# Merge gates as Strassen's seven products over pairs of feature tiles, kept in DRAM, and the branch products in a stage of their own

## The chip, the core and the metric

One core of a Trainium2 chip runs the program once. TensorE (PE) multiplies a loaded 128x128 weight tile (LDWEIGHTS, the PEld rows) with up to 512 columns into a bank of PSUM; VectorE (DVE), ScalarE (ACT) and GpSimd (POOL) do the elementwise work; SyncE (SP) issues most DMAs. The metric is the device time of one execution in microseconds (us): the median of 3 runs of the kernel before is 1403.04, and the runs lie between 1402.95 and 1403.12.

## What is computed

The reference is one layer of a network with three branches over 1024 tokens of 1024 features. Everything is float32.

```python
y = x @ w_in                  # 1024 x 1024 x N_IN, cut into the inputs of the branches
ya = attention(...)           # branch A: 512 features
yb = spatial_gating(...)      # branch B: 512 features
yc = mlstm(...)               # branch C: 512 features
merged = sum(sigmoid(gate_b) * (y_b @ w_br_b) for b in (a, b, c))   # gate_b: the last 3 x 1024 columns of y
r = ALPHA * x + merged @ w_out
r = r + sigmoid(r @ ple_gate) * (p @ ple_w)
out = layernorm(r)
```

The change concerns the merge: the gates, 3072 features of `x @ w_in` for 1024 tokens, and the three products `y_b @ w_br_b`, 512 features to 1024 each.

## The kernel before

All activations lie with features on the partitions and tokens along the free axis. A product in float32 is made of pairs: every operand is split into a rounded part (`hi`, an ACT cast to float32r) and the rest (`lo`, a DVE subtraction), and three matmuls hi*hi, lo*hi and hi*lo add up in one PSUM bank. `load_w` (L84) loads a 512 KB weight tile into `wraw`, casts it (L92) and subtracts (L93); `split` (L97) does the same to an activation tile (L102, L103); `proj_half` (L109, its matmul is L116) then makes a 128x512 result with 3 x K matmuls, K the number of 128-row feature tiles: 24 for the 8 tiles of x, 12 for the 4 tiles of a branch. x is held as 8 hi and 8 lo tiles (`xh`, `xl`, the 16 buffers of tag `x`) from the start to the end of the merge.

The program runs through these parts in this order: loading x and the compressed keys (to about 55 us of the span), attention (branch A, with projections of A and B between its steps), the gating branch B and the mLSTM branch C (their working tiles lie in the pool `pq`, L603, opened when the pool of A is closed and closed at L824), the merge (L831 to L872), the output projection (L874), and the last gate with the layer norm (L899 to L979).

The merge has a loop over the 3 branches `b`. It splits the four tiles of the branch (L837, into the pool `pf`, which is opened at L832 where `pq` was), and for each of the 8 feature tiles `n` of the output makes two gate halves (`ps_g`, L850, 24 matmuls each, with a tanh on ACT, L852) and two branch halves (`ps_b`, L858, 12 matmuls each). DVE multiplies the two (L860, L862) and for the second and third branch POOL adds the result to `M[n]` (L863). At the end `M` is split into `mh`, `ml` (L869, L870), which the output projection reads. ya, yb and yc stay in SBUF until they are split: ya and yb are the 8 buffers of tag `y`, yc the 4 of the pool `ycp`.

The order in which an engine gets its instructions is set by a scheduler at build time: it takes the program in the order written as the priority, plays it through, and gives each engine the first instruction in that order whose inputs and buffers are there. Each engine then runs its list in order and waits on semaphores. A tile waits until a buffer of its tag is free; the tiles of a pool wait for all that was done with the pools that lay at its place before.

Of the kernel before, what the change touches and what calls it, by code (L numbers as in the profile page):

```python
# [45 lines left out]
def hybrid_kernel(ctx, tc, xT, pT, wfm, wvg, wtm, cmpw1, cmpw2, cpos, vecs, sgwT, sgb,  # L46
# [32 lines left out]
    # ---------------------------------------------------------------- constants  # L79
# [3 lines left out]
    # ---------------------------------------------------------------- weights  # L83
# [22 lines left out]
    # ---------------------------------------------------------------- x  # L106
    xh, xl = [], []

    def proj_half(po, w, half, hs, ls, K=KT, M=P):  # L109
        wh, wl = w  # L110
        s = slice(half * 512, half * 512 + 512)
        n = 3 * K
        i = 0
        for k in range(K):
            for a, b in ((wh, hs), (wl, hs), (wh, ls)):
                mm(po[:M, :], lhsT=a[:, k, :], rhs=b[k][:, s], start=(i == 0), stop=(i == n - 1))  # L116
                i += 1

    def proj_tok(po, ws, tt, n, hs, ls):
        s = slice(tt * P, tt * P + P)  # L120
        i = 0
        tot = 3 * KT
        for k in range(KT):
            wh, wl = ws[k // 4]
            for a, b in ((hs, wh), (hs, wl), (ls, wh)):
                mm(po[:, :n], lhsT=a[k][:, s], rhs=b[:, k % 4, :], start=(i == 0), stop=(i == tot - 1))
                i += 1

    def proj_tok256(src, hs, ls):
        """[tokens, 256] for all token tiles, two to a bank; yields the banks in order."""  # L130
        bank = [pj(), pj(), pst("st", 2), pst("st", 2)]
        for i in range(2):
            wh, wl = load_w(src[:, 4 * i:4 * i + 4, :], 4, 256)
            for tt in range(NT):
                s = slice(tt * P, tt * P + P)
                po = bank[tt // 2][:, tt % 2 * 256:tt % 2 * 256 + 256]
                for k in range(4):
                    for j, (a, b) in enumerate(((hs, wh), (hs, wl), (ls, wh))):
                        mm(po, lhsT=a[4 * i + k][:, s], rhs=b[:, k, :],  # L139
# [16 lines left out]
    def gelu2(dst, src, n):  # L156
        """dst = 2*gelu(src) with src in PSUM or SBUF."""
# [8 lines left out]
    def silu2(dst, src, n):  # L166
        """dst = 2*silu(src)."""
# [9 lines left out]
    # ================================================================ branch A  # L177
# [21 lines left out]
    def load_x(k, parts):  # L199
        raw = yp.tile([P, T], F32, tag="y", bufs=YB, name="xraw")  # L200
        xh.append(xp.tile([P, T], F32R, tag="x", bufs=16, name="xh"))
        xl.append(xp.tile([P, T], F32R, tag="x", bufs=16, name="xl"))
        for i in range(parts):
            load_cols(raw, xT[k], (xh[k], xl[k]), slice(i * T // parts, (i + 1) * T // parts))
            if k == 0 and i == 0:
                load_kv(1, 0, 2)
# [3 lines left out]
    load_x(1, 2)  # L210
    for kv in range(2):
        load_kv(kv, 2, 8)
    for k in range(2, KT):
        load_x(k, 1)
# [19 lines left out]
    # ---- key/value streams of the compressed branch, x consumed as it arrives  # L234
# [8 lines left out]
    for k in range(KT):  # L243
        for half in range(2):
            for kv, w in enumerate((wk, wv)):
                s = slice(half * 512, half * 512 + 512)
                for i, (a, b) in enumerate(((w[0], xh), (w[1], xh), (w[0], xl))):
                    mm(pkv[kv][half], lhsT=a[:, k, :], rhs=b[k][:, s], start=(k == 0 and i == 0),
# [36 lines left out]
    # ---- values (with a column of ones) and gate logits, token-major  # L285
# [11 lines left out]
    # ---- compression  # L297
# [48 lines left out]
    def prep_group(g):  # L346
# [5 lines left out]
        for n in "sw":  # L352
            vv.tensor_scalar_mul(d["KB" + n][64:128, 0:1], xl[-1][64:128, 0:1].bitcast(F32), 0.0)
# [45 lines left out]
    def attn_front(g, qb, d):  # L399
# [3 lines left out]
        # compressed branch  # L403
# [57 lines left out]
        # row maxima of the window and of the selection  # L461
# [137 lines left out]
    # ================================================================ branch B  # L599
    pa_ctx.close()  # L600
    ycp = pool("ycp")
# [10 lines left out]
    vb = [ycp.tile([P, 2, 512], F32, tag="yc", bufs=4, name="vb") for _ in range(4)]  # L612
# [3 lines left out]
    # ================================================================ branch C  # L616
    yc = []
    # gate rows, one (head, chunk) per partition
# [29 lines left out]
    vv.tensor_scalar(out=cm, in0=cm, scalar1=mp, scalar2=None, op0=OP.max)      # u  # L648
# [15 lines left out]
    # values with ones  # L664
# [8 lines left out]
    # gating branch: normalize, mix over the chunk, gate  # L673
# [33 lines left out]

    def conv_proj(i, nm):
# [20 lines left out]
    for h in range(NH_C):  # L729
        yc.append(ycp.tile([P, T], F32, tag="yc", bufs=4, name="yc"))  # L730
# [65 lines left out]
        # gates o and z  # L796
# [18 lines left out]
        for hf in range(2):  # L815
# [7 lines left out]
            vv.tensor_mul(yc[h][:, s], pt, oz[:, s])  # L823
    pq_ctx.close()  # L824
    if "yc" in dbg:
        for i in range(4):
            nc.sync.dma_start(dbg["yc"][i], yc[i])
# [3 lines left out]
    # ================================================================ merge  # L831
    pf = pool("pf")  # L832
    M = [pf.tile([P, T], F32, tag="M", bufs=8, name="M") for _ in range(8)]
    for b, ys in enumerate((ya, yb, yc)):
        yh, yl = [], []
        for i in range(4):
            h, l = split(ys[i], pf, "s", 8)  # L837
            yh.append(h)
            yl.append(l)
        for n in range(8):  # L840
            wg = wf(FM["mg"] + 8 * b + n)
            if n % 2 == 0:
                raw = wp.tile([P, 1024], F32, tag="wraw", bufs=2, name="wraw")
                nc.sync.dma_start(raw, wbr[b, n // 2])
                wb = [t.rearrange("p (k n) -> p k n", k=8) for t in split(raw, yp, "y", YB)]
            w = (wb[0][:, 4 * (n % 2):4 * (n % 2) + 4, :], wb[1][:, 4 * (n % 2):4 * (n % 2) + 4, :])
            ts = []
            for half in range(2):
# [244 lines left out]
```

## Time and profile before

| | us |
|---|---|
| median of 3 runs | 1403.04 |
| span of the profiled execution, from its first to its last instruction (the only time of its own on the page) | 1401.3 |
| PE busy | 1383.6 (99%) |
| DVE busy | 695.8 (50%) |
| ACT busy | 430.9 (31%) |
| POOL busy | 154.7 (11%) |
| HBM read and written | 80.1 MB, 57 GB/s over the span |

The rows below give times from the start of the span. Busy time of PE counts each matmul from its issue to its modelled end, so that the times of neighbours overlap; the distance between their starts is what a matmul takes of the engine.

### The profile page before, as it was taken

What the parts mean: (1) busy time and instruction counts of PE and PEld (TensorE: products, weight loads), DVE (VectorE), ACT (ScalarE), POOL (GpSimd) and SP (SyncE); (2) the same over time, 40 slices, a digit from 0 to 9 for tenths busy, and PEclk for the clock granted to TensorE, in tenths of its full rate; (3) what the DMA queues carried; (4) which work ended last, traced back from release to release, by engine and by line L of the source; (5) the groups of instructions that cost most, each with busy time, mean ns of one, the idle gap of its engine ahead of it and who ended that gap; (6) DMA issues with size and microseconds to landing.
All of it is one profiled execution on the core that took longest, in us unless ns stands there. A gap on an engine that the chain in (4) does not pass through costs nothing. (4 is left out here: it accounts for less than half of the span.)

```text
span 1401.3 us, 18726 instructions
## 1 busy us (share of the span) xinstructions
PE 1383.6 (99%) x7375; PEld 1174.8 (84%) x7375; DVE 695.8 (50%) x1719; ACT 430.9 (31%) x875; POOL 154.7 (11%) x177
## 2 busy tenths in 40 slices
PE   9999999999999999999999999999999999999997
PEld 7978888887888999988888888888888888888886
DVE  6247677436678544575575721131123232334755
ACT  6353434243332332132332311121112122224211
POOL 0011221101211000010110000001111111000312
PEclk9999999999999999999999999999999999999999
DMA  9031111111010021021121121111111112223211
GB/s 309 31 84 31 31 35 31 39 45 42 24 34 6 16 93 46 31 76 46 61 76 46 46 62 59 45 46 45 46 46 49 57 45 89 80 83 121 87 38 46
DMA packets 26872, 81.31 MB, mean 58 GB/s; under 512 B 3480, under 2 KB 6424, under 8 KB 26784
## 3 DMA queue, kind: packets, MB, share of 16 engines
q1 hardware_dynamic: 25824, 76.96, 16.8%
q0 software_dynamic: 960, 3.15, 1.0%
q8 instruction: 58, 0.95, 0.3%
q14 instruction: 30, 0.25, 0.1%
HBM read 75.84 MB, written 4.26 MB: 57 GB/s over the span
## 5 line engine op out<-in xcount | busy, mean ns | idle before, releaser
L116 PE MATMUL ps_pj<-xh,whi 128*128 128x512 f32 x544 | 217.5, 400 | 2.3 <-DVE QA L386 2.3
L93 DVE TENSOR_TENSOR wlo<-wraw,whi 128x1024 fp32r<-128x1024 f32 x74 | 91.1, 1230 | 253.6 <-ACT whi L92 253.4
L116 PE MATMUL ps_pj<-xh,wlo 128*128 128x512 f32 x544 | 216.7, 398 | 0.0
L116 PE MATMUL ps_pj<-xl,whi 128*128 128x512 f32 x544 | 214.9, 395 | 0.0
L116 PE MATMUL ps_g<-xh,whi 128*128 128x512 f32 x384 | 149.5, 389 | 0.0
L116 PE MATMUL ps_g<-xh,wlo 128*128 128x512 f32 x384 | 149.4, 389 | 0.0
L116 PE MATMUL ps_g<-xl,whi 128*128 128x512 f32 x384 | 149.4, 389 | 0.0
L520 PEld LDWEIGHTS ps_o<-V,pt 128*128 128x128 f32 x912 | 117.1, 191 | 11.9 <-ACT pt L500 3.5
L116 PEld LDWEIGHTS ps_pj<-xh,whi 128*128 128x128 f32 x544 | 102.3, 188 | 22.7 <-PE ps_pj L116 3.9
L116 PEld LDWEIGHTS ps_pj<-xl,whi 128*128 128x128 f32 x544 | 102.4, 188 | 18.7
L116 PEld LDWEIGHTS ps_pj<-xh,wlo 128*128 128x128 f32 x544 | 102.7, 189 | 17.5
L520 PE MATMUL ps_o<-V,pt 128*128 128x65 f32 x912 | 116.2, 270 | 0.4 <-POOL pt L502 0.3
L852 ACT ACTIVATE mth<-ps_g 128x512 f32<-128x512 f32 x48 | 28.7, 597 | 253.1 <-PE ps_g L116 250.4
L500 ACT ACTIVATE pt<-ps_st 128x512 f32<-128x512 f32 x114 | 65.7, 594 | 102.0 <-PE ps_st L498 98.4
L92 ACT CAST whi<-wraw 128x1024 fp32r<-128x1024 f32 x74 | 77.3, 1045 | 49.8 <-PE ps_st L139 25.0
L116 PEld LDWEIGHTS ps_g<-xh,whi 128*128 128x128 f32 x384 | 72.1, 188 | 15.0
L116 PEld LDWEIGHTS ps_g<-xh,wlo 128*128 128x128 f32 x384 | 72.1, 188 | 14.9
L116 PEld LDWEIGHTS ps_g<-xl,whi 128*128 128x128 f32 x384 | 72.1, 188 | 14.9
L863 POOL TENSOR_TENSOR M<-M,mth 128x512 f32<-128x512 f32 x32 | 43.0, 1343 | 370.9 <-DVE mth L862 207.0
L116 PE MATMUL ps_b<-sp_hi 128*128 128x512 f32 x192 | 74.7, 389 | 0.0
L116 PE MATMUL ps_b<-sp_hi,sp_lo 128*128 128x512 f32 x192 | 74.7, 389 | 0.0
L116 PE MATMUL ps_b<-sp_lo,sp_hi 128*128 128x512 f32 x192 | 74.7, 389 | 0.0
(323 smaller groups left out, 2665.7 us busy)
## 6 DMA issues: line engine op xcount, KB each, us to landing
wraw<-in_wfm_dram SPq DMA_DIRECT2D x58, 512.0 KB, 3.5
wraw<-in_wbr_dram SPq DMA_DIRECT2D x12, 512.0 KB, 3.2
wraw<-in_wtm_dram SPq DMA_DIRECT2D x8, 512.0 KB, 3.7
wraw<-in_wout_dram SPq DMA_DIRECT2D x8, 512.0 KB, 3.3
xr<-in_xT_dram SPq DMA_DIRECT2D x8, 512.0 KB, 5.0
graw<-in_pleg_dram SPq DMA_DIRECT2D x8, 512.0 KB, 3.3
out_dram<-rtok SPq DMA_DIRECT2D x14, 256.0 KB, 2.0
xraw<-in_xT_dram SPq DMA_DIRECT2D x6, 512.0 KB, 9.3
```

The costliest lines, as they stand in the source:

```text
L92: nc.scalar.copy(hi[:, c], raw[:, c])
L93: vv.tensor_sub(lo[:, c], raw[:, c], hi[:, c])
L116: mm(po[:M, :], lhsT=a[:, k, :], rhs=b[k][:, s], start=(i == 0), stop=(i == n - 1))
L500: act(pt.rearrange("p h q -> p (h q)"), sp, AF.Exp)
L520: mm(po[:, h * 65:h * 65 + 65], lhsT=pt[:, h, :], rhs=V[:, j, vi, :], start=(first and h == 0), stop=last, skip_group_check=True)
L852: act(t, pg, AF.Tanh, scale=0.5)
L863: nc.gpsimd.tensor_add(M[n][:, s], M[n][:, s], t)
```

## The change

x comes from the host in another layout (`xm`): each of its 8 tiles holds two neighbouring feature tiles for one half of the tokens, loaded in the same order and sizes as before. The tiles of ya, yb and yc are stored to DRAM (`ysc`, 12 stores of 512 KB) when their branch is done; yc now lies in `pq`, and the pool `ycp` is gone. After `pq` is closed come two stages in place of the merge loop.

The first stage makes all gates, two output tiles at a time (12 pairs, `q`), by Strassen's scheme in Winograd's form: the weights of a pair are a 2x2 matrix of blocks (output tile by half of the features), x a 2x2 matrix (half of the features by half of the tokens), and seven products of 4 feature tiles each (12 matmuls) take the place of eight. The sums of x blocks (`T1` to `T4`) are made and split once, before the first pair; the sums of weight blocks are made and split for every product (`total`, `left`). Three of the seven results are copied out of PSUM (`kept`) because later ones go on adding into the same bank. The tanh of each gate tile is stored to DRAM (`gsc`, 24 stores of 512 KB). The second stage loads the branch tiles and the gate tiles back and makes the branch products.

```diff
+    for i in range(4):
+        nc.sync.dma_start(ysc[0][i], ya[i])
...
-            vv.tensor_mul(yc[h][:, s], pt, oz[:, s])
+            vv.tensor_mul(yc[:, s], pt, oz[:, s])
+        nc.sync.dma_start(ysc[2][h], yc)
     pq_ctx.close()
...
+    pg_ = pg_ctx.enter_context(tc.tile_pool(name="pg", bufs=1))
+    def split_op(src, pl_, tg, bf):
+        hi = pl_.tile([P, T], F32R, tag=tg, bufs=bf, name="op_hi")
+        lo = pl_.tile([P, T], F32R, tag=tg, bufs=bf, name="op_lo")
+        nc.scalar.copy(hi, src)
+        vv.tensor_sub(lo, src, hi)
+        return hi, lo
...
+    for m in range(2):
+        raws.append([yp.tile([P, T], F32, tag="y", bufs=YB, name="xraw") for _ in range(4)])
+        for t, (mm_, j) in zip(raws[m], ((m, 0), (m, 1), (m + 2, 0), (m + 2, 1))):
+            nc.sync.dma_start(t, xm[mm_, j])
+    for m in range(2):
+        b11, b12, b21, b22 = raws[m]
+        vv.tensor_sub(b11, b12, b11)
+        right["T1"][m] = split_op(b11, pg_, "t", 12)
+    for m in range(2):
+        b11, b12, b21, b22 = raws[m]
+        nc.gpsimd.tensor_sub(b12, b22, b12)
+        vv.tensor_sub(b22, b22, b11)
+        right["T2"][m] = split_op(b22, pg_, "t", 12)
+    for m in range(2):
+        b11, b12, b21, b22 = raws[m]
+        right["T3"][m] = split_op(b12, pg_, "t", 12)
+    for m in range(2):
+        b11, b12, b21, b22 = raws[m]
+        vv.tensor_sub(b21, b21, b22)
+        right["T4"][m] = split_op(b21, xp, "x", 16)
...
+        def left(src):
+            hi = pg_.tile([P, 512], F32R, tag="sh", bufs=4, name="sh")[:, 0:w]
+            lo = pg_.tile([P, 512], F32R, tag="sl", bufs=4, name="sl")[:, 0:w]
+            nc.scalar.copy(hi, src)
+            vv.tensor_sub(lo, src, hi)
...
+        def product(bank, src, name, first):
+            l = left(src)
+            for k in range(K):
+                r = [t[:, k % 2 * 512:k % 2 * 512 + 512] for t in right[name][k // 2]]
+                for i, (a, b) in enumerate(((0, 0), (1, 0), (0, 1))):
+                    mm(bank, lhsT=l[a][:, k, :], rhs=r[b], start=first and k == 0 and i == 0,
+                       stop=k == K - 1 and i == 2, skip_group_check=True)
...
+        a = pst("pj", 2, "ps_a")
+        product(a, a11, "B11", True)
+        c1 = kept(a)
+        b = pst("st", 2, "ps_b")
+        s1 = total(a21, a22, OP.add)
+        product(b, s1, "T1", True)
+        c5 = kept(b)
+        s2 = total(s1, a11, OP.subtract)
+        product(a, s2, "T2", False)
+        c2 = kept(a)
+        product(b, total(a12, s2, OP.subtract), "B22", False)
+        done(0, 1, b, c2)
+        product(a, total(a11, a21, OP.subtract), "T3", False)
+        done(1, 1, a, c5)
+        c = pst("o", 2, "ps_c")
+        product(c, a12, "B21", True)
+        done(0, 0, c, c1)
+        product(a, a22, "T4", False)
+        done(1, 0, a, None)
+    for q in range(12):
+        raw = [wp.tile([P, 1024], F32, tag=tg, bufs=bf, name="mraw") for _ in range(2)]
...
+        def done(i, j, bank, kept):
+            if kept is not None:
+                vv.tensor_add(kept, bank, kept)
+                bank = kept
+            act(gt[i][:, j * 512:j * 512 + 512], bank, AF.Tanh, scale=0.5)
+        strassen(raw[0], raw[1], 4, right, done)
+        for i in range(2):
+            nc.sync.dma_start(gsc[2 * q + i], gt[i])
+    pg_ctx.close()
     pf = pool("pf")
-    for b, ys in enumerate((ya, yb, yc)):
+    for b in range(3):
         for i in range(4):
-            h, l = split(ys[i], pf, "s", 8)
+            raw = yp.tile([P, T], F32, tag="y", bufs=YB, name="yraw")
+            nc.sync.dma_start(raw, ysc[b][i])
+            h, l = split(raw, xp, "x", 16)
         for n in range(8):
-            wg = wf(FM["mg"] + 8 * b + n)
...
-                proj_half(pg, wg, half, xh, xl)
-                t = tp.tile([P, 512], F32, tag="ge_a", bufs=2, name="mth")
-                act(t, pg, AF.Tanh, scale=0.5)
+            t = yp.tile([P, T], F32, tag="y", bufs=YB, name="gt")
+            nc.sync.dma_start(t, gsc[8 * b + n])
...
-                pb2 = pst("o", 2, "ps_b")
+                pb2 = pst(("o", "pj", "st")[(2 * n + half) % 3], 2, "ps_b")
```

The raw weight tiles of a pair use the tags `wraw`, `whi` and `wlo` in turn. `mh` and `ml` and the later gate weights move to the buffers of x, the residual tiles to tag `y`; their operations and numbers stay the same.

## Rows read from the trace of the kernel before

**Rows 1.** The page's busy times by engine, share of the span, instructions.
```profile
PE 1383.6 (99%) x7375; PEld 1174.8 (84%) x7375; DVE 695.8 (50%) x1719; ACT 430.9 (31%) x875; POOL 154.7 (11%) x177
```
**Rows 2.** Busy time by stage: stretch, its length, then PE, PEld, DVE, ACT, POOL.
```profile
595.00:793.00 198.00, 198.00 (x1014) 166.11 (x1012) 126.66 (x315) 63.20 (x137) 15.16 (x26) 1.00 0.18 56
793.00:1186.00 393.00, 393.00 (x1736) 325.55 (x1735) 104.13 (x108) 83.36 (x104) 40.83 (x31) 1.00 0.16 50
```
**Rows 3.** Groups of the merge on PE: busy us, mean ns, idle before.
```profile
L116 PE MATMUL ps_g<-xh,whi 128*128 128x512 f32 x384 | 149.5, 389 | 0.0
...
L116 PE MATMUL ps_b<-sp_hi 128*128 128x512 f32 x192 | 74.7, 389 | 0.0
```
**Rows 4.** The chain that ended last, in order of time: start, length, what.
```profile
1316.78 5.44 PE ps_g L908 x24
```
**Rows 5.** Timeline of ACT in the merge: start, length, what, [idle before <-releaser].
```profile
1097.94 0.60 ACT L852 ACTIVATE mth<-ps_g 128x512 f32<-128x512 f32 x1 [4.84 <-PE ps_g L116]
1098.43 1.04 ACT L92 CAST whi<-wraw 128x1024 fp32r<-128x1024 f32 x1
...
1114.26 0.60 ACT L852 ACTIVATE mth<-ps_g 128x512 f32<-128x512 f32 x1 [4.84 <-PE ps_g L116]
...
1121.23 2.00 ACT L869 ACTIVATE mh<-M 128x1024 fp32r<-128x1024 f32 x2
```
**Rows 6.** Timeline of PE inside attention: a projection of branch B.
```profile
460.41 0.28 PE L139 MATMUL ps_pj<-whi,xh 128*128 128x256 f32 x1
```
**Rows 7.** Groups of the whole span by shape: durations that the new operations take.
```profile
L863 POOL TENSOR_TENSOR M<-M,mth 128x512 f32<-128x512 f32 x32 | 43.0, 1343 | 370.9 <-DVE mth L862 207.0 <-issue 163.9
...
L103 DVE TENSOR_TENSOR sp_lo<-xr,sp_hi 128x512 fp32r<-128x512 f32 x16 | 11.0, 688 | 4.8 <-ACT sp_hi L102 4.8
L885 DVE SCALAR_TENSOR_TENSOR xr<-xr,ps_pj 128x512 f32<-128x512 f32 x16 | 11.0, 688 | 49.3 <-PE ps_pj L116 49.3
L102 ACT CAST sp_hi<-xr 128x512 fp32r<-128x512 f32 x16 | 9.9, 618 | 28.8 <-DVE xr L885 28.8
```
**Rows 8.** Timeline of PE where branch C ends and the merge begins.
```profile
792.59 0.60 PE L821 MATMUL ps_h<-ident,nb 128*128 128x128 f32 x4
792.94 0.48 PE L116 MATMUL ps_g<-xh,whi 128*128 128x512 f32 x1
```
**Rows 9.** Timeline of DVE at the same place.
```profile
794.38 1.22 DVE L93 TENSOR_TENSOR wlo<-wraw,whi 128x1024 fp32r<-128x1024 f32 x1
795.51 1.28 DVE L823 TENSOR_TENSOR yc<-ps_h,oz 128x512 f32<-128x512 f32 x2
798.05 3.61 DVE L103 TENSOR_TENSOR sp_lo<-ya,sp_hi 128x1024 fp32r<-128x1024 f32 x3 [1.25 <-ACT sp_hi L102]
```
**Rows 10.** Timeline of ACT at the same place.
```profile
796.96 2.00 ACT L102 CAST sp_hi<-ya 128x1024 fp32r<-128x1024 f32 x2 [3.08 <-DVE yc L823]
```
**Rows 11.** Waits of SP's queue: who for whom, us in total, times, longest.
```profile
SPq L605 <- PE ps_ot L535: 40.8, 1, 40.8
```
**Rows 12.** DMA issues: KB each, median us from issue to landing.
```profile
wraw<-in_wfm_dram SPq DMA_DIRECT2D x58, 512.0 KB, 3.5
...
out_dram<-rtok SPq DMA_DIRECT2D x14, 256.0 KB, 2.0
```
**Rows 13.** A stretch of the tail, where PE is done; after POOL: PEclk, DMA share, GB/s.
```profile
1391.00:1393.00 2.00, 0.01 (x1) 0.00 (x0) 1.43 (x4) 0.38 (x1) 0.00 (x0) 1.00 0.00 0
...
1395.00:1397.00 2.00, 0.00 (x0) 0.00 (x0) 1.97 (x3) 0.00 (x0) 1.30 (x1) 0.80 0.00 0
```
**Rows 14.** Timeline of PE at the start of the span.
```profile
1.51 3.59 PE L183 MATMUL ps_m<-warm 128*128 128x512 bf16 x8 [1.51 <-DVE warm L179]
...
6.61 0.57 PE L248 MATMUL ps_pj<-xh,whi 128*128 128x512 f32 x1
7.02 0.39 PE L248 MATMUL ps_st<-xh,wlo 128*128 128x512 f32 x1
7.25 0.39 PE L248 MATMUL ps_st<-xl,whi 128*128 128x512 f32 x1
```

More of the change, by code (lines that the diff above doesn't have):

```diff
@@ L175, in wf @@
         return load_w(wfm[i], KT, P, parts)
+    ysc = [[dr.tile([P, T], F32, name=f"ysc{b}{i}") for i in range(4)] for b in range(3)]
+    gsc = [dr.tile([P, T], F32, name=f"gsc{n}") for n in range(24)]
     warm = tp.tile([P, 512], F32, tag="zz", bufs=1, name="warm")
@@ L611, in hybrid_kernel @@
     nc.sync.dma_start(bsb, sgb.to_broadcast([P, 512]))
-    vb = [ycp.tile([P, 2, 512], F32, tag="yc", bufs=4, name="vb") for _ in range(4)]
+    vb = [pq.tile([P, 2, 512], F32, tag="yc", bufs=4, name="vb") for _ in range(4)]
     for wi in range(2):
@@ L706, in hybrid_kernel @@
         return
+    for i in range(4):
+        nc.sync.dma_start(ysc[1][i], yb[i])
     def conv_proj(i, nm):
@@ L729, in hybrid_kernel @@
     for h in range(NH_C):
-        yc.append(ycp.tile([P, T], F32, tag="yc", bufs=4, name="yc"))
+        yc = pq.tile([P, T], F32, tag="yc", bufs=4, name="yc")
         k2 = conv_proj(4 + h, "k2")
@@ new lines, in hybrid_kernel @@
+    right = {n: [None, None] for n in ("T1", "T2", "T3", "T4")}
+    raws = []
+    for m in range(2):
[11 more added lines that the diff above has]
+        right["T2"][m] = split_op(b22, pg_, "t", 12)
@@ new lines, in hybrid_kernel, with strassen, total, kept @@
+    for m in range(2):
[5 more added lines that the diff above has]
+        right["T4"][m] = split_op(b21, xp, "x", 16)
+    for n, m, j in (("B11", 0, 0), ("B21", 2, 0), ("B22", 2, 1)):
+        right[n] = [(xhs[m + r][j], xls[m + r][j]) for r in range(2)]
+    def strassen(raw0, raw1, K, right, done):
+        w = K * P
+        a11, a12, a21, a22 = raw0[:, 0:w], raw0[:, w:2 * w], raw1[:, 0:w], raw1[:, w:2 * w]
+        def left(src):
[3 more added lines that the diff above has]
+            vv.tensor_sub(lo, src, hi)
+            return hi.rearrange("p (k n) -> p k n", k=K), lo.rearrange("p (k n) -> p k n", k=K)
+        def total(x, y, op):
+            t = pg_.tile([P, 512], F32, tag="ss", bufs=4, name="ss")[:, 0:w]
+            vv.tensor_tensor(out=t, in0=x, in1=y, op=op)
+            return t
+        def product(bank, src, name, first):
[5 more added lines that the diff above has]
+                       stop=k == K - 1 and i == 2, skip_group_check=True)
+        def kept(bank):
+            t = pg_.tile([P, 512], F32, tag="cp", bufs=4, name="cp")
+            nc.scalar.copy(t, bank)
+            return t
+        a = pst("pj", 2, "ps_a")
[17 more added lines that the diff above has]
+        done(1, 0, a, None)
@@ new lines, in hybrid_kernel @@
+    WTAGS = (("wraw", 2), ("whi", WB), ("wlo", WB))
+    for q in range(12):
+        tg, bf = WTAGS[q % 3]
+        raw = [wp.tile([P, 1024], F32, tag=tg, bufs=bf, name="mraw") for _ in range(2)]
+        for i in range(2):
+            nc.sync.dma_start(raw[i], wfm[FM["mg"] + 2 * q + i])
+        gt = [yp.tile([P, T], F32, tag="y", bufs=YB, name="gt") for _ in range(2)]
+        def done(i, j, bank, kept):
[4 more added lines that the diff above has]
+        strassen(raw[0], raw[1], 4, right, done)
+        for i in range(2):
+            nc.sync.dma_start(gsc[2 * q + i], gt[i])
@@ L878, in hybrid_kernel @@
         w = load_w(wout[n], KT, P)
-        xr = pf.tile([P, T], F32, tag="s", bufs=8, name="xr")
-        nc.sync.dma_start(xr, xT[n])
+        xr = yp.tile([P, T], F32, tag="y", bufs=YB, name="xr")
+        nc.sync.dma_start(xr.rearrange("p (j t) -> p j t", j=2),
+                          xm[n // 2, :, :, n % 2 * 512:n % 2 * 512 + 512].rearrange("j p t -> p j t"))
         for half in range(2):
@@ L912, in hybrid_kernel @@
         if k in (2, 3):
-            raw = pf.tile([P, T], F32, tag="s", bufs=8, name="graw")
+            raw = yp.tile([P, T], F32, tag="y", bufs=YB, name="graw")
         else:
@@ L916, in hybrid_kernel @@
         nc.sync.dma_start(raw, pleg[k])
[L917 removed]
+        h, l = split2(raw, k == 0, xp, "x", 16)
         gh.append(h)
```

93 lines of the change are left out of this document (44 added, 49 removed).

## The prediction

> **What bounds the kernel now.** I read the busy times first. PE is busy for 99% of the span, DVE for half of it, ACT for a third [rows 1]. Then the stages: in the merge, 793 to 1186 us, PE is busy for all 393 us, DVE for 104 and ACT for 83 [rows 2]. So the merge lasts as long as its matmuls need, and only fewer matmuls, or gaps between them, can move it. What one costs isn't its mean duration: the groups of the merge show 389 ns and no idle time before them [rows 3], but those durations overlap. In the chain that ended last, 24 matmuls of 128x512 take 5.44 us [rows 4], 0.2267 us each. The merge keeps this pace: from a gate's tanh to the same tanh of the next tile there are 16.32 us [rows 5] for 72 matmuls, again 0.2267. The 389 ns would price everything below 1.7 times too high.
>
> **The change, part by part.**
>
> *Matmuls removed.* A pair of gate tiles had 2 x 2 x 24 = 96 matmuls; seven products of 4 tiles have 7 x 12 = 84. Twelve pairs save 144 of 1152, and 144 x 0.2267 = 32.6 us. The 576 of the branches stay. The Trainium skill prices this otherwise: "TensorE: Matmul & The Clock Gate", section "Back-to-back issue gap", gives some 131 ns as the sustained spacing of load and matmul pairs at 512 columns (and 216 ns for one apart). By 131 ns the saving would be 18.9 us. The trace disagrees, at 227 ns in both places, and the measured spacing decides.
>
> *Elementwise work added per pair.* A pair lasts 84 x 0.2267 = 19.0 us. On ACT: 7 casts of 0.62 [rows 7], 3 copies out of PSUM and 4 tanhs of 0.60 each [rows 5], 8.5 us. On DVE: 7 subtractions and 4 sums of 0.69, and 3 additions with PSUM of 0.69 [rows 7], 9.7 us. Both lie beside PE if an engine isn't made to wait in the wrong place. Written out, each product's cast stands behind the copy of the product before, which waits for PE. But the order written is only a priority: a projection of branch B that is written after all of attention runs inside it, at 460 us [rows 6], and the first cast of M, written after the merge, runs in it at 1121 [rows 5]. The weight sums depend on a DMA alone and have 4 buffers, so casts should run up to 4 products (10.9 us) ahead of PE. A copied bank is used again one product (2.72 us) later, and the copy takes 0.60. I take 0 for the steady state; were the cover gone, a product would cost the copy 0.60, cast 0.62 and subtraction 0.69, 1.9 us (bounds 0 and 1.9).
>
> *The start of the new stage.* Here a cover is lost. Before, PE goes from the last transposes of branch C (792.59) straight on to a gate of the merge at 792.94 [rows 8], since x and the weights lie in pools that are open throughout. What goes into the new pool waits: the split of ya, long ready, begins at 796.96, released by the last product that makes yc [rows 10], which ends at 796.79 [rows 9]; PE had 10.9 us of gates to do meanwhile. At the other change of pools a load waited 40.8 us on SP for the last transpose of attention [rows 11]. In the changed kernel even the first product needs a split weight from the new pool, so PE has nothing from 792.94 on. The steps: yc is done at 795.6, as the weight subtraction of 1.22 that now stands before it goes [rows 9]. Its store must land before `pq` is released. No 512 KB store is in the trace: stores of 256 KB take 2.0 us and loads of 512 KB 3.5 [rows 12]; I take 3.5 for the size, with 2.0 and 5 as ends, and the pool opens at 799.2. Then the casts: T1, T2 and T3 stand before the first weight in the order written, 6 tiles. (T4 goes into buffers of x that are free by 790, and the differences themselves need only loads into tag `y`, free since B: both fall into C, where DVE has 71 of 198 us left [rows 2].) On ACT 6 casts take 6 x 1.0 [rows 10] and the weight's 0.62; DVE follows 1.1 behind and is slower: 6 x 1.20 [rows 9, 10], then 0.69 for the weight. So the second matmul, which needs that, can start at 799.2 + 1.1 + 7.2 + 0.7 = 808.2. Without the gap it would have started at 793.2: 15.0 us lost. With the pool opening at 797.7 or 800.7 it is 13.5 or 16.5.
>
> *The clock after it.* The granted clock is a mean 0.80 of full between 1395 and 1397 [rows 13]: at its lower level, 1.2 GHz, from about 1396.2, 5.2 us after PE's last work. At the start matmuls come 0.41 us apart up to 7.0 and 0.23 from there on [rows 14]: 5.5 us at the lower level after the first warm-up matmul at 1.51, half of which is lost. A gap of 15 us is longer than the 5.2, so I add 2.7 us (bounds 0 and 5.5).
>
> *The second stage.* 576 matmuls, 130.6 us. Per output tile, 5.44 us of PE: POOL 2 x 1.34 and DVE 2 x 0.69 [rows 7], with 1.2 for its share of splits at 1.22 a tile. Even taking turns that is 5.3, under PE. Loads are some 1 MB per tile; at 3.5 us per 512 KB one after the other [rows 12] that is 7, but they have several buffers, and run beside each other. The first tiles are split while the last pair still runs, in the buffers that its early products free. Nothing lost; bounds 0 and 3.
>
> *The rest, at nothing.* The stores of ya and yb add 8 issues to SP, those of ya before the loads that branches B and C begin with; at 0.33 us each that is 1.3 us for the start of B, beside the projections that PE has there. The layout of x alters no size at the start. The last four splits of M now wait for buffers that the last branch product frees; PE has 10.9 us of output matmuls to fill with, of which half need only the first four. Bounds of the three together: -0.4 and +2.
>
> *Sum.* -32.6 + 15.0 + 2.7 = -14.9. Against the profiled span of 1401.3 that makes 1386.4; the median of the runs is 1.7 above that span, so 1388.1. About 0.2%, 2.8 us, is what a measurement of this kernel can tell from no change.
>
> **The rivals.**
>
> *A smaller gap.* If the scheduler puts the first weight before the six splits, or splits of x needn't wait, PE starts 0.62 + 0.69 after the pool opens, at 800.5: 7.3 lost in place of 15.0, 1380.4. Against it: the order written. 0.13.
>
> *A larger gap.* If the differences of x aren't made during C, because the buffers of `y` come free late or DVE has no room, DVE has 6 x 1.22 = 7.3 us more to do after the pool opens: 1395.4. For it: yb leaves its buffers only after its own store. Against it: 200 us lie between. 0.13.
>
> *Products that wait for the copy before them (slower).* If the casts stand in ACT's list where they are written, PE waits 1.9 us at each of 84 products: 160 us, 1548. Even one per pair would give 12 x 1.9 = 23, 1411; it decides from 8 stalls on, where 8 x 1.9 uses up the gain of 14.9. For it: in the merge the next weight's cast stands right behind a tanh that waited 4.84 us for PE, 1098.43 [rows 5], although its buffer is free sooner. Against it: the overtaking in rows 5 and 6. 0.10.
>
> *Even.* The saving is there but nearly all given back, by a gap and a second stage at their upper bounds together (16.5 + 5.5 + 3 + 2 = 27.0 of 32.6, 1397.4) and a few stalls more. By the spacing in the Trainium skill it would come out here too: 18.9 less 17.7. 0.06.
>
> **How the numbers follow.** The forecast of 1388.1 gets 0.58; with the bounds of store, clock and second stage its own range is 1384 to 1394. The cases of a smaller and a larger gap, 0.13 each, are faster as well: 0.84 faster, 0.06 same, 0.10 slower. The range from 1379 to 1397 takes in the forecast and both gaps, and leaves out even and slower, 0.16 together, and a little at the edges.
>
> **What would show it.** Right: 1008 gate matmuls, 0.227 us apart, 84 in 19.0 us from pair to pair; one gap of PE of about 15 us after the transposes of C, ended by a DVE subtraction, with the granted clock at half in it and for a few us after; a stage from the first gate to the last branch product of 359 us and a little. Wrong: PE idle before each product or each pair, ended by ACT or DVE; branch products waiting for DMA or POOL; a gap under 8 us or over 20.

## The result and the profile after

The changed kernel takes 1386.12 us (median of 4 runs, 1385.80 to 1387.18) against 1403.05 (1402.95 to 1403.12): a ratio of 0.9882, with a 95% interval of 0.9868 to 0.9896. Forecast were 1388.1. Its profiled execution has a span of 1384.3, 17.0 less than before, and its own time, 1386.04, is 1.7 above that.

The page's busy times and two groups, to be held against [rows 1] and [rows 3]:

```profile
PE 1355.4 (98%) x7231; PEld 1148.0 (83%) x7231; DVE 804.4 (58%) x1882; ACT 484.9 (35%) x974; POOL 162.1 (12%) x179
...
L907 PE MATMUL ps_a<-op_hi,sh 128*128 128x512 f32 x144 | 56.0, 389 | 0.0
...
L894 DVE TENSOR_TENSOR sl<-ss,sh 128x512 fp32r<-128x512 f32 x48 | 33.1, 692 | 35.2 <-ACT sh L893 34.9
```

144 matmuls are gone (7375 to 7231), and DVE has 109 us more to do. Busy time by stage, columns as in [rows 2]: branch C, the gates, the branch products, the first output tiles.

```profile
595.00:795.00 200.00, 199.10 (x1016) 166.44 (x1014) 132.55 (x319) 64.93 (x138) 20.46 (x27) 1.00 0.26 85
795.00:1035.00 240.00, 232.15 (x1015) 191.30 (x1013) 127.83 (x181) 106.76 (x178) 0.00 (x0) 0.98 0.31 112
1035.00:1165.00 130.00, 130.00 (x574) 107.19 (x574) 68.81 (x75) 28.81 (x29) 40.67 (x31) 1.00 0.62 211
1165.00:1178.00 13.00, 11.79 (x54) 9.14 (x52) 8.52 (x9) 3.65 (x5) 2.14 (x1) 1.00 0.13 42
```

PE is idle for 0.9 us in this part of branch C, for 7.85 in the gate stage, for 1.2 at the start of the output, and nowhere among the branch products. PE's timeline at the end of C and where the gates begin, and then the first matmul of the seventh product (T4) in the first and in the second pair:

```profile
794.19 1.04 PE L840 MATMUL ps_h<-ident,nb 128*128 128x128 f32 x8
802.40 0.79 PE L907 MATMUL ps_a<-xh,sh 128*128 128x512 f32 x1 [7.17 <-ACT sh L893]
803.87 0.79 PE L907 MATMUL ps_b<-op_hi,sh 128*128 128x512 f32 x1 [0.67 <-ACT sh L893]
804.46 0.63 PE L907 MATMUL ps_a<-xh,sl 128*128 128x512 f32 x1
...
822.00 0.39 PE L907 MATMUL ps_a<-op_hi,sh 128*128 128x512 f32 x1
...
841.04 0.39 PE L907 MATMUL ps_a<-op_hi,sh 128*128 128x512 f32 x1
```

From pair to pair there are 841.04 - 822.00 = 19.04 us for 84 matmuls, 0.2267 each: the pace of before, with nothing between. All that is lost is lost at the start. The chain of that stretch, in order of time, tells how:

```profile
797.93 2.60 DMA ysc<-yc
...
800.78 1.05 ACT op_hi L857
801.83 0.52 ACT sh L893
802.35 0.95 ACT op_hi L857
803.30 0.53 ACT sh L893
...
803.87 0.79 PE ps_b L907
804.66 3.95 PE ps_a L907 x11
808.61 2.49 PE ps_b L907 x11
```

The store of the last yc lands, the pool opens at 800.8, and the casts of x and of weights take turns; 11 matmuls then take 3.95 us, and the next 11 take 2.49. The windows beside it give the granted clock (the third number from the right):

```profile
795.00:802.00 7.00, 0.23 (x3) 0.00 (x0) 3.99 (x6) 1.22 (x2) 0.00 (x0) 0.67 0.59 226
802.00:804.00 2.00, 0.93 (x2) 0.42 (x2) 2.00 (x4) 2.00 (x4) 0.00 (x0) 0.50 0.00 0
804.00:808.00 4.00, 4.00 (x11) 3.14 (x12) 4.00 (x5) 3.17 (x4) 0.00 (x0) 0.55 0.00 0
808.00:811.00 3.00, 3.00 (x15) 2.48 (x14) 2.39 (x3) 1.54 (x2) 0.00 (x0) 1.00 0.00 0
```

Where the 17.0 us come from, stage by stage, before and after, by starts of PE's matmuls:

| stretch | before | after | difference |
|---|---|---|---|
| start of the span to the first matmul of C (`ps_m`) | 574.09 | 574.86 | +0.8 |
| from there to the last transpose of C | 218.83 | 220.09 | +1.3 |
| gates and branch products | 391.81 | 370.00 | -21.8 |
| output projection up to its first transpose | 11.82 | 12.67 | +0.8 |
| the rest | 204.70 | 206.63 | +1.9 |

The first line is within the scatter: the code of that part is the same in the changed kernel and all twelve below, whose profiles show 574.06 to 575.83. Of the kernel before there is one profile, at the low end of these, so a small cost of the new stores there can't be told from scatter.

### The profile page after: what moved, and what is told of

Read it like the earlier page. It is cut to its first block, busy times and chain, and to the rows that moved or that the text cites. A ratio compares the mean times of both kernels' runs of the same rounds, so it can differ in the third digit from the quotient of the medians.

```text
span 1384.3 us, 18935 instructions
## 1 busy us (share of the span) xinstructions
PE 1355.4 (98%) x7231; PEld 1148.0 (83%) x7231; DVE 804.4 (58%) x1882; ACT 484.9 (35%) x974; POOL 162.1 (12%) x179
## 5 line engine op out<-in xcount | busy, mean ns | idle before, releaser
L129 PEld LDWEIGHTS ps_pj<-xl,whi 128*128 128x128 f32 x544 | 102.4, 188 | 18.9
L979 POOL TENSOR_TENSOR M<-M,gt 128x512 f32<-128x512 f32 x32 | 42.8, 1349 | 350.4 <-DVE gt L978 334.8
L129 PE MATMUL ps_b<-sp_hi,wlo 128*128 128x512 f32 x192 | 74.7, 389 | 0.0
L129 PE MATMUL ps_b<-sp_hi,whi 128*128 128x512 f32 x192 | 74.7, 389 | 0.0
L129 PE MATMUL ps_b<-sp_lo,whi 128*128 128x512 f32 x192 | 74.1, 390 | 0.0
L907 PE MATMUL ps_a<-op_hi,sh 128*128 128x512 f32 x144 | 56.0, 389 | 0.0
L907 PE MATMUL ps_a<-op_hi,sl 128*128 128x512 f32 x144 | 56.0, 389 | 0.0
L907 PE MATMUL ps_a<-op_lo,sh 128*128 128x512 f32 x144 | 56.0, 389 | 0.0
L1024 PE MATMUL ps_g<-gh,sp_hi 128*128 128x512 f32 (+1 forms) x144 | 52.7, 366 | 0.0
L1024 PE MATMUL ps_g<-gh,sp_lo 128*128 128x512 f32 (+1 forms) x144 | 52.7, 366 | 0.0
L1024 PE MATMUL ps_g<-gl,sp_hi 128*128 128x512 f32 (+1 forms) x144 | 52.6, 366 | 0.0
```

Source lines behind the costliest of these rows:

```text
L129: mm(po[:M, :], lhsT=a[:, k, :], rhs=b(k, half), start=(i == 0), stop=(i == n - 1))
L907: mm(bank, lhsT=l[a][:, k, :], rhs=r[b], start=first and k == 0 and i == 0, stop=k == K - 1 and i == 2, skip_group_check=True)
L979: nc.gpsimd.tensor_add(M[n][:, s], M[n][:, s], t[:, s])
L1024: mm(po[:, 0:n], lhsT=a[k][:, ts_], rhs=b[k][:, s], start=(k == 0 and i == 0), stop=(k == KT - 1 and i == 2))
```

## The experiments

"Gate stage" is the time from the last transpose of C to the first branch matmul, and "lost" is that less 0.2267 for each of its matmuls (1008, or 1152 in plain8). Ratios are to the kernel before. Each length is read from one profile: c_tail and m_in_s, which leave the gate stage as it is, show 239.14 and 239.82 against 239.20, so some 0.7 us between two gate stages tell nothing. The runs of fill24, t1_in_x and fill_t1 overlap with those of the changed kernel.

| kernel | median us | ratio, 95% interval | C | gate stage | lost |
|---|---|---|---|---|---|
| changed kernel | 1386.12 | 0.9882, 0.9868 to 0.9896 | 220.09 | 239.20 | 10.7 |
| plain8 | 1415.15 | 1.0087, 1.0071 to 1.0102 | 218.93 | 269.98 | 8.8 |
| ahead1 | 1534.66 | 1.0938, 1.0916 to 1.0960 | 220.05 | 387.70 | 159.2 |
| need_order | 1384.37 | 0.9866, 0.9851 to 0.9881 | 220.04 | 237.67 | 9.2 |
| fill24 | 1385.32 | 0.9877, 0.9861 to 0.9894 | 220.09 | 238.82 | 10.3 |
| t1_in_x | 1387.22 | 0.9887, 0.9873 to 0.9902 | 220.15 | 238.91 | 10.4 |
| fill_t1 | 1386.67 | 0.9885, 0.9869 to 0.9902 | 220.15 | 240.18 | 11.7 |
| yc_out | 1393.86 | 0.9936, 0.9921 to 0.9951 | 218.80 | 248.63 | 20.1 |
| early2 | 1380.46 | 0.9837, 0.9822 to 0.9852 | 220.16 | 233.70 | 5.2 |
| early3 | 1378.37 | 0.9824, 0.9810 to 0.9839 | 220.17 | 231.47 | 3.0 |
| c_tail | 1385.00 | 0.9872, 0.9855 to 0.9888 | 218.93 | 239.14 | 10.7 |
| m_in_s | 1390.93 | 0.9911, 0.9896 to 0.9925 | 220.11 | 239.82 | 11.3 |
| sum3 | 1375.52 | 0.9802, 0.9788 to 0.9815 | 219.03 | 231.44 | 3.0 |

**Is it the seven products? (plain8)**

```diff
-        a = pst("pj", 2, "ps_a")
-        product(a, a11, "B11", True)
...
+        for i, (x1, x2) in enumerate(((a11, a12), (a21, a22))):
+            ls = [left(x1), left(x2)]
+            for j in range(2):
+                bank = pst("st" if j else "pj", 2, "ps_a")
+                for r in range(2):
+                    product(bank, ls[r], f"B{r + 1}{j + 1}", r == 0, r == 1)
+                done(i, j, bank, None)
```

> The two stages, the stores to DRAM and the loads back stay, but each pair makes eight plain products from four split weight blocks (each used for two halves of the tokens) in place of seven; the sums of x, their splits, the sums of weights and the copies are gone. If the gain is the matmuls removed, this kernel has 144 more than the changed one, 144 x 0.2267 = 32.6 us more, less what the gap before the first product shrinks: with no splits of x to make, PE should start some 2 us after the pool opens and lose about 8 us in place of 10.5. Also gone is the subtraction on POOL in branch C, 1.2 us. So 1386.1 + 32.6 - 2.5 - 1.2 = 1415, 12 us slower than the kernel before: the price of the new stages by themselves. The rival, that the two stages save time by their own order (branch products apart from the gates), says 1403 or less.

1415.15, as expected. PE's timeline has the same matmul of two neighbouring pairs, 96 matmuls apart, at

```profile
824.13 0.39 PE L885 MATMUL ps_a<-xh,sh 128*128 128x512 f32 x1
...
845.89 0.39 PE L885 MATMUL ps_a<-xh,sh 128*128 128x512 f32 x1
```

That is 21.76 us for a pair, where the seven products take 19.04: 12 x 2.72 = 32.6, as forecast. The whole gate stage is 30.8 us longer, with PE idle for 6.22 us in it in place of 7.85. The stages by themselves cost 12 us against the kernel before; the gain comes from the products alone.

**What hides the elementwise work? (ahead1)**

```diff
-            hi = pg_.tile([P, 512], F32R, tag="sh", bufs=4, name="sh")[:, 0:w]
-            lo = pg_.tile([P, 512], F32R, tag="sl", bufs=4, name="sl")[:, 0:w]
+            hi = pg_.tile([P, 512], F32R, tag="sh", bufs=1, name="sh")[:, 0:w]
+            lo = pg_.tile([P, 512], F32R, tag="sl", bufs=1, name="sl")[:, 0:w]
```

> The split weight blocks of the seven products have one buffer each (tags sh and sl) in place of four, so the next product's cast can start only when PE has done the product before. Theory: the casts running ahead are what hides the elementwise work, so each of 84 products now waits for the cast (0.62) and the subtraction (0.69), 1.3 us plus semaphores, and where the cast stands behind a copy out of PSUM or a tanh another 0.6: 84 x 1.3 to 1.9 = 109 to 160 us, 1495 to 1546, with PE idle before each product and DVE (sl) named as what ended it. The rival, that PE would not have waited in any case because a hi part and a lo part are needed at different times (the cast alone counts, 0.62), says about 84 x 0.7 = 59, 1445. If nothing waits, 1386.

1534.66. Between two products, in the timeline of all engines:

```profile
903.01 0.39 PE L907 MATMUL ps_a<-xl,sh 128*128 128x512 f32 x1
903.43 0.59 ACT L912 COPY cp<-ps_a 128x512 f32<-128x512 f32 x1 [3.60 <-PE ps_a L907]
903.91 0.62 ACT L893 CAST sh<-ss 128x512 fp32r<-128x512 f32 x1
904.57 0.69 DVE L894 TENSOR_TENSOR sl<-ss,sh 128x512 fp32r<-128x512 f32 x1 [4.01 <-ACT sh L893]
904.59 0.49 PE L907 MATMUL ps_b<-op_hi,sh 128*128 128x512 f32 x1 [1.19 <-ACT sh L893]
...
905.31 0.50 PE L907 MATMUL ps_b<-op_hi,sl 128*128 128x512 f32 x1 [0.23 <-DVE sl L894]
```

The copy waits for PE, the cast stands behind the copy, and the second matmul waits for the subtraction: the steps of the slower rival, forced here by the buffers and not by the order on ACT. It costs (387.70 - 239.20) / 84 = 1.77 us a product, where the forecast had 1.9. In the changed kernel four buffers keep this chain off PE.

**The gap: order, clock or DVE? (need_order, fill24, t1_in_x, fill_t1)** The first writes the splits of T1 to T4 where a product first needs them:

```diff
-        right["T1"][m] = split_op(b11, pg_, "t", 12)
...
+    lazy["T1"] = lambda: [split_op(r[0], pg_, "t", 12) for r in raws]
...
             l = left(src)
+            if name in lazy:
+                right[name] = lazy.pop(name)()
```

> The splits of T1 to T4 are written where the first pair needs them (T1 after the first product's weights, and so on) in place of all ahead of the first pair. Theory: in the changed kernel the first weight's cast stood second on ACT behind one split of x, and its second matmul waited for a DVE subtraction that stood behind x's; with the weight first, PE starts dense about 2 us earlier, but product 2 then waits for T1, whose four tile operations on ACT and DVE take 2 x 1.0 and 2 x 1.2: it is needed 2.7 to 5 us after the first weight. Expected 1384 to 1385.5, the first product's second matmul at about 802 in place of 803.9. The rival, that the opening of the pool (800.8) and the clock alone set the gap, says 1386.

As expected: the first product's second matmul starts at 802.33 (804.46 in the changed kernel; the 803.9 of the expectation is the first matmul of the second product), and 9.2 are lost in place of 10.7. So some 1.5 us of the loss is order. plain8, which has no x to split at all, still loses 8.8: what is left is the wait for the pool, one weight, and the clock.

```diff
+    pfill = pst("m", 2, "ps_fill")
+    for i in range(24):
+        mm(pfill, lhsT=xhs[0][0][:, 0:P], rhs=xhs[0][0][:, 0:512], start=True, stop=True)
```

> 24 matmuls of 128x512 whose result is not used (a tile of x by itself) follow the last transposes of branch C and keep PE busy for 24 x 0.2267 = 5.4 us of the 7.4 in which it has nothing to do. Theory: the part of the loss that comes from the clock, 11 matmuls at 0.363 us in place of 0.227 plus a few before them, 1.5 to 2 us, returns: 1384.3, with 0.227 between the matmuls of the first product. The rival, that those matmuls are slow because of their operands, says 1386 with the same 0.363.

The clock stayed at its upper level (first row below, columns as above), the first product's matmuls came 0.23 apart, and yet the stage is only 0.4 us shorter, no more than scatter. PE caught up with its suppliers and waited for them once more at the fourth and fifth product, which it hadn't done before (second row, PE's timeline).

```profile
804.00:808.00 4.00, 4.00 (x19) 3.31 (x18) 3.98 (x6) 3.32 (x5) 0.00 (x0) 1.00 0.00 0
```

```profile
812.77 0.50 PE L911 MATMUL ps_a<-op_hi,sh 128*128 128x512 f32 x1 [0.63 <-ACT sh L897]
```

So I took work from DVE: T1 into the buffers that T4 had, T4 into the new pool.

```diff
-        right["T1"][m] = split_op(b11, pg_, "t", 12)
+        right["T1"][m] = split_op(b11, xp, "x", 16)
...
-        right["T4"][m] = split_op(b21, xp, "x", 16)
+        right["T4"][m] = split_op(b21, pg_, "t", 12)
```

> T1 takes the four buffers of x that T4 had, which are free by 790 us, and T4 goes into the new pool. So T1's splits run during C, and only T2 and T3 stand before the first products once the pool is open. Theory (DVE's splits set when PE is dense, since holding the clock up gave 0.4 us of a possible 1.9 and ended in waits for DVE at the third and fourth product): two splits of 1.2 less in front of PE, so the stage from the end of C to the first branch product is 2 to 2.4 us shorter than 239.2: 1384. The rival, that the clock sets it, leaves 239 and 1386.

A miss: the stage is 0.3 us shorter, again no more than scatter, not 2. The split that is next in the order simply took the place of T1's ahead of the first weight, and its subtraction the place on DVE (the first `sl` at 803.30, 803.18 in the changed kernel). Both edits together:

> The 24 unused matmuls that hold the clock, and T1 in x, together. Each alone left the stage from the last transpose of C to the first branch product nearly as long as the changed kernel's 239.2 us (238.8 and 238.9). Theory: two limits end within a us of each other, the half clock and DVE's list of splits, so that either one alone uncovers the other; with both eased the stage takes 237 to 237.6 and the kernel 1384. The rival, that neither matters and the weight's split sets it all, leaves 238.8.

Inconclusive: though the 24 matmuls ran, the clock fell this time (0.53 from 804.5 to 808), so the two weren't eased together, and 11.7 us were lost.

**The gap: open the pool sooner, or do without it? (yc_out, early2, early3)** On top of T1 in x, the last yc goes into a `y` buffer:

```diff
+        if h == NH_C - 1:
+            yc = yp.tile([P, T], F32, tag="y", bufs=YB, name="yc")
...
```

> As the kernel with T1 in x, and the last tile of yc lies in a tag y buffer, not in the pool that is closed, so the pool opens when yc is made and not when its 512 KB store has landed (2.8 us). Theory: the first cast on ACT starts at about 798 in place of 800.8, released by DVE and not by a DMA, and the stage is 2.8 us shorter than with T1 in x alone: 1381. The rival, that loads queued behind the store or the loads of weights (mraw) are late instead, gives less than 1 us.

The pool did open sooner: the first weight's cast starts at 795.96, released by DVE's product, and PE's first matmul at 796.63. But the loads of x, of which the last four left SP from 597.42 to 600.40 in the changed kernel, were all issued only now (SP's timeline up to 800, where one of the eight is still to come, then PE's):

```profile
792.91 0.42 SPq L869 DMA_DIRECT2D xraw<-in_xm_dram x1
...
796.20 3.89 SPq L869 DMA_DIRECT2D xraw<-in_xm_dram x6
```

```profile
805.78 0.80 PE L910 MATMUL ps_b<-op_hi,sh 128*128 128x512 f32 x1 [4.13 <-ACT op_hi L860]
```

All differences of x fell behind the end of C, and 20.1 us were lost, 9.7 more than in t1_in_x. This is the rival of the larger gap, which had priced 7.3, without the loads. What the sooner opening is worth by itself isn't shown, since the loads moved with it. That the loads wait because the buffers of one tag are handed out in the order written, in which yc comes ahead of x, is the likely reason; it wasn't tried by itself. Nothing needs the pool to open sooner if the first products don't use it:

```diff
+            if early:
+                h2, l2, i = early.pop(0)
+                hi, lo = h2[:, i * 512:i * 512 + 512], l2[:, i * 512:i * 512 + 512]
...
+        if q == 0:
+            eh2 = wp.tile([P, 1024], F32R, tag="whi", bufs=WB, name="eh2")
+            el2 = wp.tile([P, 1024], F32R, tag="wlo", bufs=WB, name="el2")
+            early = [(eh2, el2, 0), (eh2, el2, 1)]
```

> The first pair's first two products need nothing from the new pool: their split weights take buffers of tags whi and wlo, the sum of weights one of the temporaries, T1 the buffers of x, and the splits of T2 to T4 are written where they are needed. Theory (the gap is there only because the first weights and sums wait for the pool): PE goes from the transposes of C straight into 24 matmuls, 5.4 us, and then waits 2 to 4 us for T2's splits after the pool opens at 800.8; the clock stays up. The stage's loss falls from 10.7 to 4 us or less: 1379 to 1381. The rival, that ACT and DVE can't make the early weights during C, leaves the first matmul at 802 and 1384.

1380.46, as expected, but with 5.2 us lost in place of 4 or less, and the clock didn't stay up. PE's timeline goes from C's transposes straight into 24 matmuls, then waits 2.58 us, and 0.24 a little later:

```profile
795.23 1.03 PE L840 MATMUL ps_h<-ident,nb 128*128 128x128 f32 x8
796.01 0.47 PE L914 MATMUL ps_a<-xh,eh 128*128 128x512 f32 x1
...
804.33 0.50 PE L914 MATMUL ps_a<-op_hi,sh 128*128 128x512 f32 x1 [2.58 <-ACT op_hi L857]
```

Of the 5.2 us, 1.6 are lost at half clock (8 matmuls in 3.39 us from 806.41). A third product that needs no sum of x fills the wait:

```diff
+        c = None
+        if early:
+            c = pst("o", 2, "ps_c")
+            product(c, a12, "B21", True)
```

> As the kernel that makes its first two products before the pool opens, with a third one: the product of the block B21 of x, which needs no sum, is moved up to third place for the first pair, its weight's halves in a second pair of whi and wlo buffers. There PE still waited 3.0 us for T2 and then ran some 11 matmuls at half clock, 5.2 us lost in all. Theory: 2.7 us more of work that needs nothing of the pool covers the wait, the clock stays up, and about 1 us is lost: a stage of 229.5, 1376. The rival, that DVE, which has the sums, the weights and T2 to T4 to split from 801.7 on, is then late for the products that follow, loses 3 or more: 1378 or above.

1378.37, as the rival had it. The clock stays up, as the theory said, but 3.0 us are lost, most of it around three waits of 0.30, 0.82 and 0.78 for ACT and DVE; two of them, in PE's timeline:

```profile
805.45 0.50 PE L914 MATMUL ps_a<-op_lo,sh 128*128 128x512 f32 x1 [0.82 <-DVE op_lo L858]
...
814.25 0.50 PE L914 MATMUL ps_a<-op_hi,sh 128*128 128x512 f32 x1 [0.78 <-DVE cp L961]
```

**The terms put at nothing (c_tail, m_in_s, sum3).** In C, T3's subtraction stands on POOL ahead of the products `qe`, which began at 613.34 before. POOL's timeline of the changed kernel, then PE, which waited for them:

```profile
612.88 3.37 POOL L873 TENSOR_TENSOR xraw<-xraw 128x1024 f32<-128x1024 f32 x1 [0.97 <-DVE xraw L869]
616.21 4.77 POOL L763 TENSOR_TENSOR qe<-q,eb 128x256 f32<-128x256 f32 x4
```

```profile
616.99 0.49 PE L791 MATMUL ps_n<-C,qe 128*128 128x129 f32 x2 [0.90 <-POOL qe L763]
```

At the start of the output, and in the tail, PE waits for M's last splits and for a tile of p that goes through the two buffers of `wraw`:

```profile
1170.79 0.50 PE L129 MATMUL ps_pj<-mh,whi 128*128 128x512 f32 x1 [0.91 <-ACT mh L984]
...
1172.05 0.50 PE L129 MATMUL ps_pj<-ml,whi 128*128 128x512 f32 x1 [0.30 <-DVE ml L985]
...
1286.44 0.50 PE L1064 MATMUL ps_e<-gh 128*128 128x512 f32 x1 [0.97 <-ACT gh L1018]
```

c_tail moves the subtraction to DVE, and two more tiles of the last gate's weights, which share `wraw` with those of p, to tag `y` (this expectation and that of sum3 call the moved tiles p tiles; the edit leaves those of p in `wraw`):

```diff
-        nc.gpsimd.tensor_sub(b12, b22, b12)
+        vv.tensor_sub(b12, b22, b12)
...
-        if k in (2, 3):
+        if k in (2, 3, 4, 5):
```

> Two small edits away from the gap. In branch C the subtraction that makes T3 moves from POOL to DVE: there it took 3.37 us beside a DVE subtraction of 4.77 us, and a matmul waited 1.2 us behind it. In the last stage the second pair of p tiles is loaded through tag y too, so that four of them no longer wait for two buffers of wraw, where PE waited 1.35 us once. Theory: C ends 1.2 us earlier and the tail is 1 to 1.9 us shorter, with the gap as it is: 1383. The rival, that DVE in C has no room and delays another step, and that the wait in the tail turns up at the next matmul, says 1386.

C is 220.09 - 218.93 = 1.2 us shorter, as expected, and as long as in plain8 and yc_out, which make no differences there: the whole +1.3 was this one place on POOL. The part behind the first output transpose went from 206.6 to 206.0, less than the 1 to 1.9 expected; kernels without this edit show 206.2 to 207.0, so this gain is hardly clear of scatter. The wait for p stays, at 1.106 us between two starts in place of 1.354.

```diff
-            h, l = split(raw, xp, "x", 16)
+            h, l = split(raw, *((pf, "s", 12) if b == 2 else (xp, "x", 16)))
```

> Only the end of the second stage differs from the changed kernel: the tiles of the third branch are split into the buffers of tag s, which lie idle there, so that x's buffers are free for all eight splits of M as soon as M's tiles are done. In the changed kernel three casts of M (2.96) and their DVE subtractions (2.73) started only when the last branch product freed their buffers, and PE then waited 1.08 and 0.46 us in the first output tile. Theory: those waits shrink to 0.5 or less: 1385, the output projection's first tile 1 us shorter. The rival, that the last tile's chain (DVE, POOL 2.14, ACT, DVE) sets the wait whatever the buffers do, leaves 1.5 us of waits and 1386.

A miss, and a costly one: 4.8 us slower than the changed kernel. With their buffers free, the splits of M stood in DVE's list ahead of the products of the next tile, and the last tile's two products were made only at 1167.20, behind a split that had waited for ACT (at 1162.44 and 1166.69 in the changed kernel). PE then waited 2.75 us for `mh`, and the clock fell once more. DVE's timeline:

```profile
1166.06 1.23 DVE L985 SCALAR_TENSOR_TENSOR ml<-M,mh 128x1024 fp32r<-128x1024 f32 x1 [3.19 <-ACT mh L984]
1167.20 1.28 DVE L978 SCALAR_TENSOR_TENSOR gt<-gt,ps_b 128x512 f32<-128x512 f32 x2
```

Neither price came out. What the rival said of the cause does show: the last tile's chain still ends right before PE's wait does, POOL's addition at 1171.51, the cast behind it at 1172.60, PE's matmul at 1172.65. sum3 is early3 with c_tail's edits and one step of that chain on another engine:

```diff
-                    nc.gpsimd.tensor_add(M[n][:, s], M[n][:, s], t[:, s])
+                    (vv if (b, n, half) == (2, 7, 1) else nc.gpsimd).tensor_add(M[n][:, s], M[n][:, s], t[:, s])
```

> The kernel that makes three products before the pool opens, with three small edits: T3's subtractions on DVE in place of POOL (C ended 1.6 us earlier with it), the second pair of p tiles and two more through tag y (tail 0.6 us shorter), and the very last addition to M, that of the half which ends the second stage, on DVE in place of POOL, where it took 2.14 us beside DVE's work and the cast that PE then waited for stood behind it. Theory: 1.2 to 1.6 us from C, 0.6 from the tail, and 0.5 to 1 from the wait of 1.08 us in the first output tile: 1378.4 - 2.5 = 1376. The rival, that each of these waits uncovers the next one, as it was when M's splits were given free buffers, leaves 1378.

1375.52, near the theory's 1376 and the fastest of all, 27.6 us below the kernel before. The page's busy times and DVE's timeline at the end of the branch products:

```profile
PE 1353.7 (99%) x7231; PEld 1146.2 (83%) x7231; DVE 802.8 (58%) x1885; ACT 484.3 (35%) x974; POOL 155.2 (11%) x176
```

```profile
1159.81 0.68 DVE L1002 TENSOR_TENSOR M<-M,gt 128x512 f32<-128x512 f32 x1
1160.42 1.21 DVE L93 TENSOR_TENSOR wlo<-wraw,whi 128x1024 fp32r<-128x1024 f32 x1
```

The stretch up to the first output transpose fell from 12.67 to 11.61. Of the 32.6 us that the seven products are worth, 27.6 are now there; 3.0 are lost in the first pair, and 1.3 behind the first output transpose (206.0 against 204.7).

## Why the prediction was right, and where it was not

- *Matmuls removed, -32.6.* Right: a pair takes 19.04 us, against 21.76 with eight products in plain8, 32.6 for twelve pairs. The spacing of 131 ns that the Trainium skill gives ("TensorE: Matmul & The Clock Gate", section "Back-to-back issue gap"), which would have made 18.9 of it, didn't appear.
- *Steady state, 0.* Right, with its cover named: 0.2267 between starts from 808.45 on. ahead1 takes the cover away and finds the price, 1.77 a product, near the upper bound of 1.9. The chain of the slower rival is real, and with four buffers it doesn't reach PE; whether the order on ACT alone could bring it about wasn't tried.
- *The gap, +15.0.* The chain is right (store, pool, split, weight), its size is not: without the clock it is 10.7 - 1.5 = 9.2, and PE's 7.85 us of idle time lie under the 8 that I had named as a sign of being wrong. The trace names casts on ACT as what ended both waits, 7.17 and 0.67 us, where I had a DVE subtraction; that one (`sl`) ends at 803.87, when the second wait does. The step that failed is "T1, T2 and T3 stand before the first weight in the order written, 6 tiles": on ACT the first weight stood second, at 801.83 in the chain, not seventh. I took the order written as binding among all that was ready; of the six splits in my sum one stood ahead of the weight. Why the scheduler put it second the trace doesn't tell. The smaller gap, the rival with 0.13, was so the nearer account: it had PE at work 1.3 us after the pool opens and 7.3 lost. The first matmul came 1.6 after, the next 3.1 after, where the forecast had 9.0, and 9.2 were lost, where it had 15.0.
- *The store, 3.5.* It took 2.60, inside its bounds of 2.0 to 5.
- *The clock, +2.7.* 1.5: 11 matmuls in 3.95 us in place of 2.49. I had compared the gap with the 5.2 us after which the clock fell at the end of the span. Here it fell sooner: a mean of 0.67 from 795 to 802, all of it at 1.00 or 0.50, puts the fall at 797.4, 2.1 us after PE's last transpose ended (795.23).
- *The second stage, 0.* Right: 130.8 us from its first matmul to the first of the output, against 130.6.
- *The rest, at nothing, -0.4 to +2.* Wrong: 1.3 + 0.8 + 1.9 = 4.0. Of the 1.9, which scatters by 0.8 between kernels, 1.1 is the one wait for p (1.354 between two starts in place of 0.227); the rest stays open. I had named DVE's room in C, but not POOL's queue, with `qe` behind the subtraction. M's last splits I covered with 10.9 us of output matmuls "of which half need only the first four", and left out that the last tile's chain runs over four engine steps. "Their operations and numbers stay the same" was true of the tail, but their buffers did not stay the same.
- *The sum.* -14.9 forecast, -17.0 measured. The gap and its clock were 17.7 - 10.7 = 7.0 too dear, and what I had put at nothing, with the 0.8 of scatter ahead of C, was 4.8 too cheap: that the forecast came within 2.0 us owes something to these two misses cancelling. The bounds of store, clock and second stage add up to 1388.1 + 1.5 + 2.8 + 3 = 1395.4, not to the 1394 that I gave.
- *A larger gap.* It didn't come, since the loads of x were issued by 600.40. yc_out shows its cost where they weren't: with the differences of x behind the end of C, 20.1 us are lost.

## What to carry to other kernels

Fewer matmuls on a bound engine pay at their measured spacing, if the next operand is ready some products ahead; price the chain that would appear without that, since it is what a buffer too few costs. Where a stage begins in a new pool, look at what its first operations need: what helped here was to let the first products lie in buffers that were already there, while the one try at opening the pool sooner held up the loads of x. Before an elementwise step goes to an idle engine or to other buffers, read what is queued behind it there, since two such moves here, T3's subtraction on POOL (1.2 us) and M's splits in free buffers (4.8), cost more than they could save.

## What the runs showed of the hardware

*The clock fell within the long wait, and some time after short ones.* In the changed kernel it was at its lower level (0.50 from 802 to 804) before PE was back from the wait of 7.17 us. In fill_t1 PE worked until 800.5, waited 1.71 us, did one matmul, waited 0.97 and was then busy; the granted clock was 1.00 up to 804.5 and at the lower level only then (0.53 from 804.5 to 808). In fill24 the same waits (1.68 and 0.97) brought no fall. In early2 a wait of 2.58 us was followed by two us of work, with 0.24 of waiting in it, and then by 3.4 us at 0.51; early3, with waits of 0.30 and 0.82, kept 1.00. The matmuls at the lower level lost 1.5 us in the changed kernel and 1.6 in early2, and after the same waits the fall came in one profile and not in the other.

*POOL and DVE hold each other up.* Where the second stage ends, in the changed kernel (DVE, then POOL):

```profile
1167.29 1.21 DVE L985 SCALAR_TENSOR_TENSOR ml<-M,mh 128x1024 fp32r<-128x1024 f32 x1
1168.42 2.31 DVE L93 TENSOR_TENSOR wlo<-wraw,whi 128x1024 fp32r<-128x1024 f32 x1
```

```profile
1163.26 1.29 POOL L979 TENSOR_TENSOR M<-M,gt 128x512 f32<-128x512 f32 x1 [1.43 <-issue]
1167.51 2.14 POOL L979 TENSOR_TENSOR M<-M,gt 128x512 f32<-128x512 f32 x1 [2.96 <-DVE gt L978]
```

POOL's addition takes 1.29 by itself and 2.14 here: 1.29 after DVE's first operation ends, 1168.50, makes 1169.8, and it ends at 1169.65. DVE's next takes 2.31: 1.21 after 1169.65 makes 1170.9, and it ends at 1170.73. With the addition on DVE, in sum3, that subtraction takes 1.21. The Trainium skill, "SBUF — State Buffer", section "SBUF: two separate sides", says that DVE instructions with two SBUF inputs and GpSimd's share a pair of ports which the first holds for its whole instruction while the other blocks; these rows agree to 0.2 us.
